# Encoder block on one core: weights of four stages moved to 112 bytes from the left factor

## The chip, the cores and the metric

The kernel runs on one core of a Trainium2 chip. The metric is device time in microseconds of one execution; the kernel before took 948.29 us (median of three runs, 947.97 to 948.39).

## The reference

One layer of an encoder, 256 tokens of width 2048, all in float32:

```python
h = rmsnorm(x, norm1_g)
q, k, v, u = split(h @ w_in)              # 12 q heads, 4 k/v heads of 128; u 512 wide
a = rmsnorm(window_attention(q, k, v, sink), attn_out_g)      # |t-s| <= 128, ALiBi, sink
f = rmsnorm(fourier_mix(u, w_fourier), fourier_out_g)         # Re(DFT2), then a map per group
x = x + concat([a, f]) @ w_out
h = rmsnorm(x, norm2_g)
gate, val = split(h @ w_up)               # 5504 columns each
gate = depthwise_conv3(gate, dw_w) + dw_b
x = x + (gelu(gate) * val) @ w_down
y = rmsnorm(x, normf_g)
```

## The kernel before, in words

Every large matmul is done in three parts to keep float32 precision: each operand is split into a rounded half `hi` (float32r) and the rest `lo`, and hi*hi, lo*hi and hi*lo are summed in PSUM. Weights come in units of 128 x 2048 values. `load` brings a unit to SBUF through SP's queue, three units ahead; `split` makes the halves two units ahead of their use, `hi` with a copy on ScalarE (ACT, line 168) and `lo` with a subtraction on VectorE (DVE, line 169). `parts_of` gives the halves their slots: three slots of 2176 elements for each of `hi` and `lo`, and inside the slot the 2048 values start at an offset that `shifts` names for the unit. Offsets count elements of 4 bytes.

TensorE takes two operands. The left factor is loaded into the array (LDWEIGHTS, PEld in the profile), then the other operand streams through it, up to 512 columns for one matmul. Two helpers use the weights in the two roles:

- `moving_weights` (lines 302 to 304) streams the weights, and the left factor is a 128-column piece of activations: `hT` for u and v, `cat` for the output projection, `act` for the late k tiles of the down projection. The first four k tiles of u (line 381) and the last k tiles of the down projection (`last_product`, lines 1190 to 1192) do the same with loops of their own.
- `still_weights` (line 319) takes the weights as left factor and streams the activations: q, k, gate and val.

The stages follow each other in an order that the program writes out by hand: u (units 0 to 3, `ps_u`), v (4 to 7, `ps_v`), q and k (16 units) with attention and Fourier work between them, the output projection (16 units, `ps_a` and `ps_ff`), gate and val (86 units) and between them the down projection. The down projection of the first 32 k tiles is done by seven products of blocks instead of eight (`split_product`, `by_parts`, lines 1051 to 1053, tiles `ps_P` and `ps_N`), where `hi` and `lo` stream and the operands `op_P`, `op_N` are left factors. The other k tiles are "late" (32 to 39, `ps_l`, two groups of four units) and "last" (40 to 42, `ps_e`, made by `split_last` and the line 168 splits).

Where the operands lie in SBUF is plain from the built program. The slots of `hi`, `lo`, `cat`, `act` and `op` start at byte 32 modulo 128, `hT` at byte 96. The table gives the start of the streamed operand minus the start of the left factor, modulo 128 bytes, before the change:

| matmuls | offset in the slot | distance |
|---|---|---|
| u, v | 16 elements (64 bytes) | 0 |
| q, k, gate, val | hi 0, lo 16 elements, as left factor | hi 64, lo 0 |
| output projection | 0 | 0 |
| products of the down projection | 28 elements (112 bytes) | 112 |
| late and last k tiles of the down projection | 0 | 0 |

Of the kernel before, what the change touches and what calls it, by code (L numbers as in the profile page):

```python
# [9 lines left out]
F32R = mybir.dt.float32r  # L10
# [3 lines left out]
P = 128  # L14
# [20 lines left out]
SHIFT = 16  # L35

PRODUCT_SHIFT = 28

V_G2, V_GA, V_GF, V_DW, V_DB, V_SINK = 0, 16, 28, 32, 161, 204
V_N = 216  # L40
# [52 lines left out]
def block_kernel(  # L93
# [26 lines left out]
    def f32(ap):  # L120
        return ap.bitcast(F32)
# [4 lines left out]

    units = [(w_u_x[i], 2048) for i in range(4)] + [(w_in[i], 2048) for i in range(20)]
    units += [(w_out[i], 2048) for i in range(16)]
    shifts = [(SHIFT, SHIFT)] * 8 + [(0, SHIFT)] * 16 + [(0, 0)] * 16
    n_front = len(units)  # L130
    items, up_index = ff_items(), {}
    for n, it in enumerate(items):
        if it[0] == "product":
            continue
        up_index[n] = len(units)
        if it[0] in ("gate", "val"):
            units.append((w_up[2 * it[1] + (it[0] == "val")], 2048))
            shifts.append((0, SHIFT))
            continue
        elif it[0] == "down":  # L140
            units.append((w_down_late[4 * it[1] + it[2]], 2048))
        else:
            units.append((w_down_last[it[1]], 512 * len(LAST)))
        shifts.append((0, 0))
    RAW = 3
    raws, halves = {}, {}

# [6 lines left out]
    def parts_of(i):  # L154
        halves[i] = tuple(
            wp.tile([P, 2176], F32R, tag=h, name=f"{h}{i}", bufs=3)[:, s : s + 2048]
            for h, s in zip(("hi", "lo"), shifts[i])
        )
        return halves[i]
# [44 lines left out]
    def u_part(k, o, n, m=1):  # L204

        rows = ux[k // 4][:, (k < 4) * U_HEAD :].rearrange("p (k c) -> p k c", k=4)
        return rows[:, k % 4 : k % 4 + m, o : o + n]
# [155 lines left out]
    for k in range(NK):  # L363
        c, q = k // 4, k % 4
        if q == 0:
            hi, lo = (t.rearrange("p (k c) -> p k c", k=4) for t in parts_of(c))
        n = 1 if c < 2 else 2
# [3 lines left out]
        if q % n == 0:  # L371
            w, h = u_part(k, 0, FW, n), hi[:, q : q + n, :]
# [416 lines left out]
    for n, (c, kq) in enumerate(OUT_ORDER):  # L789
        i = N_OUT + n  # L790
# [32 lines left out]
    fp = ctx.enter_context(tc.tile_pool(name="fp", bufs=2))  # L823
# [106 lines left out]
    def split_product(g, c, p):  # L930
# [5 lines left out]
            wp.tile([P, 2176], F32R, tag=h, name=f"{h}_{p}_{g}{c}", bufs=3)[  # L936
                :, PRODUCT_SHIFT : PRODUCT_SHIFT + 2048
            ]
# [192 lines left out]
    for n, it in enumerate(items):  # L1131
# [15 lines left out]
        if it[0] == "product":  # L1147
            kind, g, c, p = it
# [10 lines left out]
        else:  # L1159
            kind, g, c = it  # L1160
            hi, lo = halves.pop(up_index[n])
# [11 lines left out]
    i = up_index[n]  # L1173

    def split_last(c):
        raw, n = raws[i + c], 512 * len(LAST)
        hi = fp.tile([P, 2048], F32R, tag="rawd", name=f"hi{i + c}")
        lo = fp.tile([P, 2048], F32R, tag="rawd", name=f"lo{i + c}")
        halves[i + c] = (hi, lo)
        nc.scalar.activation(hi[:, 0:n], raw[:, 0:n], AF.Copy)  # L1180
        nc.vector.tensor_tensor(lo[:, 0:n], raw[:, 0:n], f32(hi[:, 0:n]), ALU.subtract)

    def last_product(c, b, o=0, n=512):
# [11 lines left out]
        last_post(c, b, ps, o, n)  # L1195

    split_last(3)
    for c in range(4):
        last_product(c, 0)
# [122 lines left out]
```

## Time and profile before

| what | value |
|---|---|
| median of three runs | 948.29 us |
| the profiled execution | 947.67 us |
| its span, first to last instruction | 945.9 us |
| TensorE busy, mean granted clock | 936.5 us (99%), 0.997 |
| weight loads, VectorE, ScalarE busy | 812.6, 749.6, 534.0 us |

In time the stages stand so, in us from the span's start: u to 27, v to 53, q, k and attention to 161, output projection to 256 (its first units between the last attention steps), gate, val and products to 845, late tiles from 845 to 867 and from 899 to 921, last tiles to 938, final norm and output to 946. The profile models the ends of matmuls, and they overlap in the array, so TensorE's pace is read from one start to the next.

### The profile page before, as it was taken

The numbers are of one execution on the slowest core, as the hardware profiler recorded it, in microseconds if no ns is written. First come the engines' busy times: TensorE is split into PE (matmuls) and PEld (weight loads), VectorE is DVE, ScalarE is ACT, GpSimd is POOL, SyncE is SP. The second block draws the span as 40 slices with busy tenths as digits, with TensorE's granted clock in tenths as the row PEclk, the third lists the DMA queues.
The fourth block names the chain that finished last, engine by engine and source line by source line (L and its number), as shares of the span: only waits on it lengthen the run. The fifth ranks groups of instructions, "written<-read, shape, count | busy, mean of one in ns | idle before, by whom it ended". The sixth has DMA issues, their size and how long they took to land.

```text
span 945.9 us, 12778 instructions
## 1 busy us (share of the span) xinstructions
PE 936.5 (99%) x5085; PEld 812.6 (86%) x5085; DVE 749.6 (79%) x935; ACT 534.0 (56%) x646; POOL 42.0 (4%) x57
## 2 busy tenths in 40 slices
PE   9999999999999999999999999999999999999996
PEld 7889998888888888888888888888888888888885
DVE  7758877666676689787898877988879979888776
ACT  7656766455454546556565555665556755553442
POOL 0000000000000000000000000000000000000002
PEclk9999999999999999999999999999999999999998
DMA  9854444446546675978778797877987697776542
GB/s 367 337 185 144 168 146 166 142 170 222 178 178 227 251 234 187 287 244 265 225 260 245 241 304 235 267 231 229 294 257 243 209 298 222 222 244 218 182 134 89
DMA packets 32108, 211.58 MB, mean 224 GB/s; under 512 B 3504, under 2 KB 4016, under 8 KB 7984
## 3 DMA queue, kind: packets, MB, share of 16 engines
q1 hardware_dynamic: 28448, 184.55, 52.6%
q0 software_dynamic: 3600, 26.22, 14.6%
q8 instruction: 40, 0.66, 0.3%
q14 instruction: 20, 0.16, 0.0%
HBM read 208.65 MB, written 2.10 MB: 223 GB/s over the span
## 4 chain that ended last, share of the span: by engine, by line
PE 98%; issue 1%; DMA 0%; DVE 0%; POOL 0%; ACT 0%; DVEq 0%; POOLq 0%; ACTq 0%
PE ps_gate L319 25%; PE ps_val L319 25%; PE ps_q L319 7%; PE ps_P L1051 3%; PE ps_P L1053 3%; PE ps_P L1052 3%; PE ps_a L304 2%; PE ps_k L319 2%; PE ps_a L302 2%; PE ps_a L303 2%; PE ps_N L1051 2%; PE ps_N L1053 2%; PE ps_N L1052 2%; PE ps_l L303 2%; PE ps_l L302 2%; PE ps_l L304 2%
## 5 line engine op out<-in xcount | busy, mean ns | idle before, releaser
L169 DVE TENSOR_TENSOR lo<-raw,hi 128x2048 fp32r<-128x2048 f32 (+1 forms) x133 | 302.6, 2275 | 54.3 <-ACT hi L168 54.3
L168 ACT ACTIVATE hi<-raw 128x2048 fp32r<-128x2048 f32 (+1 forms) x133 | 253.1, 1903 | 59.5 <-PE ps_l L303 24.9
L319 PE MATMUL ps_gate<-hU,hi 128*128 128x512 f32 x688 | 236.2, 389 | 0.0
L319 PE MATMUL ps_val<-hU,hi 128*128 128x512 f32 x688 | 236.2, 389 | 0.0
L319 PE MATMUL ps_gate<-hU,lo 128*128 128x256 f32 x688 | 189.9, 276 | 0.0
L319 PE MATMUL ps_val<-hU,lo 128*128 128x256 f32 x688 | 189.9, 276 | 0.0
L319 PEld LDWEIGHTS ps_gate<-hU,hi 128*128 128x128 f32 x688 | 129.2, 188 | 26.8
L319 PEld LDWEIGHTS ps_val<-hU,hi 128*128 128x128 f32 x688 | 129.1, 188 | 26.8
L319 PEld LDWEIGHTS ps_gate<-hU,lo 128*128 128x128 f32 x688 | 129.2, 188 | 1.1
L319 PEld LDWEIGHTS ps_val<-hU,lo 128*128 128x128 f32 x688 | 129.2, 188 | 1.1
L831 ACT ACTIVATE ft_g<-ps_gate 128x256 f32<-128x256 f32 x43 | 16.5, 384 | 120.1 <-PE ps_gate L319 119.9
L831 ACT ACTIVATE ft_v<-ps_val 128x256 f32<-128x256 f32 x43 | 16.5, 384 | 88.1 <-PE ps_val L319 88.1
L319 PE MATMUL ps_q<-hT,hi 128*128 128x512 f32 x192 | 66.2, 392 | 0.0
L319 PE MATMUL ps_q<-hT,lo 128*128 128x256 f32 x192 | 52.3, 277 | 0.0
L1053 PE MATMUL ps_P<-lo_P,op_P 128*128 128x512 f32 x128 | 49.8, 389 | 0.0
L1051 PE MATMUL ps_P<-hi_P,op_P 128*128 128x512 f32 x128 | 49.8, 389 | 0.0
L1052 PE MATMUL ps_P<-hi_P,op_P 128*128 128x512 f32 x128 | 49.8, 389 | 0.0
L943 DVE TENSOR_TENSOR lo_N<-sumw,hi_N 128x2048 fp32r<-128x2048 f32 x16 | 36.6, 2290 | 10.2 <-ACT hi_N L942 10.2
L319 PEld LDWEIGHTS ps_q<-hT,hi 128*128 128x128 f32 x192 | 35.7, 188 | 6.9
L302 PE MATMUL ps_a<-hi,cat 128*128 128x512 f32 x96 | 37.9, 395 | 0.0
L304 PE MATMUL ps_a<-lo,cat 128*128 128x512 f32 x96 | 37.5, 391 | 0.0
L833 DVE TENSOR_TENSOR fa_g<-ps_gate,ft_g 128x256 f32<-128x256 f32 x43 | 18.1, 421 | 24.3 <-ACT ft_g L831 24.3
(332 smaller groups left out, 1603.0 us busy)
## 6 DMA issues: line engine op xcount, KB each, us to landing
raw<-in_w_up SPq DMA_DIRECT2D x86, 1024.0 KB, 5.1
raw<-in_w_in SPq DMA_DIRECT2D x20, 1024.0 KB, 4.8
raw<-in_w_out SPq DMA_DIRECT2D x16, 1024.0 KB, 4.8
sumw<-in_w_down POOLq DMA_DIRECT2D x16, 1024.0 KB, 8.6
raw<-in_w_down_late SPq DMA_DIRECT2D x8, 1024.0 KB, 4.8
raw<-in_w_down_last SPq DMA_DIRECT2D x4, 768.0 KB, 4.2
ux<-in_w_u_x SPq DMA_DIRECT2D x3, 768.0 KB, 9.0
xs<-in_x SPq DMA_DIRECT2D x4, 512.0 KB, 16.3
```

Of the source, the lines that this page charges most:

```text
L168: nc.scalar.activation(hi[:, 0:n], raw[:, 0:n], AF.Copy)
L169: nc.vector.tensor_tensor(lo[:, 0:n], raw[:, 0:n], f32(hi[:, 0:n]), ALU.subtract)
L302: nc.tensor.matmul(ps, ah, wh, start=first and q == q0, stop=False)
L303: nc.tensor.matmul(ps, al, wh, start=False, stop=False)
L304: nc.tensor.matmul(ps, ah, wl, start=False, stop=last and q == q0 + len(kk) - 1)
L319: nc.tensor.matmul(ps[:, x], (hi, lo)[i][:, k * P : (k + 1) * P], hk(k)[:, x], start=n == 0 and k == 0, stop=n == len(order) - 1 and k == ...
L831: nc.scalar.activation(tmp, ps[:, S : 2 * S], AF.Copy)
L833: nc.vector.tensor_tensor(add, ps[:, 0:S], tmp, ALU.add)
L943: nc.vector.tensor_tensor(lo, src, f32(hi), ALU.subtract)
L1051: nc.tensor.matmul(ps, o[:, 0, p, :], hi[:, s], start=first and p == 0, stop=False)
L1052: nc.tensor.matmul(ps, o[:, 1, p, :], hi[:, s], start=False, stop=False)
L1053: nc.tensor.matmul(ps, o[:, 0, p, :], lo[:, s], start=False, stop=last and p == 3)
```

## The change

Every unit whose weights stream gets the offset that makes its distance 112 bytes. For u and v that is 44 elements (176 bytes from the slot's start, 112 from `hT` modulo 128), for the output projection and the late and last tiles 28 elements. The tiles of `split_last` are cut the same way. The gate, val, q and k units and the products are left as they are. Slots, their sizes and addresses, the order of instructions, transfers and waits are the same in both programs; the start of `hi` and `lo` differs in 849 matmuls, 42 ScalarE and 46 VectorE instructions, each time by 28 elements. For the last tile, `hi` and `lo` of `split_last`, the slots are those of `rawd`.

```diff
+FRONT_SHIFT = SHIFT + PRODUCT_SHIFT
...
-    shifts = [(SHIFT, SHIFT)] * 8 + [(0, SHIFT)] * 16 + [(0, 0)] * 16
+    shifts = [(FRONT_SHIFT, FRONT_SHIFT)] * 8 + [(0, SHIFT)] * 16
+    shifts += [(PRODUCT_SHIFT, PRODUCT_SHIFT)] * 16
...
-        shifts.append((0, 0))
+        shifts.append((PRODUCT_SHIFT, PRODUCT_SHIFT))
...
     def split_last(c):
         raw, n = raws[i + c], 512 * len(LAST)
-        hi = fp.tile([P, 2048], F32R, tag="rawd", name=f"hi{i + c}")
-        lo = fp.tile([P, 2048], F32R, tag="rawd", name=f"lo{i + c}")
+        hi, lo = (
+            fp.tile([P, 2048], F32R, tag="rawd", name=f"{h}{i + c}")[
+                :, PRODUCT_SHIFT : PRODUCT_SHIFT + n
+            ]
+            for h in ("hi", "lo")
+        )
```

## The prediction

> **What bounds the kernel now.** I read the page first, then the groups with their forms kept apart, then TensorE's timeline at the places that the change touches, then the busy times by stage.
>
> ```profile
> span 945.9 us, 12778 instructions
> ...
> PE 936.5 (99%) x5085; PEld 812.6 (86%) x5085; DVE 749.6 (79%) x935; ACT 534.0 (56%) x646; POOL 42.0 (4%) x57
> ...
> PEclk9999999999999999999999999999999999999998
> ...
> PE 98%; issue 1%; DMA 0%; DVE 0%; POOL 0%; ACT 0%; DVEq 0%; POOLq 0%; ACTq 0%
> ```
>
> TensorE is busy for 99% of the span, at full granted clock, and the chain that ended last is 98% TensorE. Beside the matmuls the weight loads (PEld) run for 86% of the span: nearly always one operand streams through the array while the next left factor is being read. So the kernel takes as long as its matmuls take from start to start, and a change of addresses can matter on one path above all: if it alters that step. The busy durations don't show the step, as matmuls overlap; the starts in the timeline do. First a product, whose streamed operand already lies 112 bytes (modulo 128) from its left factor:
>
> ```profile
> 360.84 0.39 PE L1051 MATMUL ps_P<-hi_P,op_P 128*128 128x512 f32 x1
> ...
> 363.33 0.39 PE L1053 MATMUL ps_P<-lo_P,op_P 128*128 128x512 f32 x1
> 363.56 0.39 PE L319 MATMUL ps_val<-hU,hi 128*128 128x512 f32 x1
> ```
>
> Twelve matmuls lie between 360.84 and 363.56: 2.72 / 12 = 226.7 ns each, from the first one on. Now the four places that the change moves, all at a distance of 0 modulo 128 so far: u, the output projection, and the late tiles of the down projection (v has the addresses of u).
>
> ```profile
> 10.60 0.39 PE L302 MATMUL ps_u<-hi,hT 128*128 128x512 f32 x1
> ...
> 13.32 0.39 PE L302 MATMUL ps_u<-hi,hT 128*128 128x512 f32 x1
> ...
> 219.35 0.39 PE L303 MATMUL ps_a<-hi,cat 128*128 128x512 f32 x1
> ...
> 238.62 0.40 PE L304 MATMUL ps_a<-lo,cat 128*128 128x512 f32 x1
> ...
> 845.00 0.39 PE L302 MATMUL ps_l<-hi,act 128*128 128x512 f32 x1
> ...
> 846.15 0.39 PE L304 MATMUL ps_l<-lo,act 128*128 128x512 f32 x1
> 846.38 0.39 PE L302 MATMUL ps_l<-hi,act 128*128 128x512 f32 x1
> ...
> 850.46 0.39 PE L302 MATMUL ps_l<-hi,act 128*128 128x512 f32 x1
> ```
>
> u: 12 matmuls in 2.72 us, 226.7 ns. Output projection: 85 in 19.27 us, 226.7 ns. Late tiles: 18 from 846.38 to 850.46 in 4.08 us, 226.7 ns. In steady flow distance 0 and distance 112 have the same step to a tenth of a nanosecond. That is the row on which the forecast rests.
>
> What remains above this step shows in the groups: the mean is 389 ns where nothing is in the way, and larger where a matmul's successor came late.
>
> ```profile
> L1051 PE MATMUL ps_P<-hi_P,op_P 128*128 128x512 f32 x128 | 49.8, 389 | 0.0
> ...
> L302 PE MATMUL ps_a<-hi,cat 128*128 128x512 f32 x96 | 37.9, 395 | 0.0
> L304 PE MATMUL ps_a<-lo,cat 128*128 128x512 f32 x96 | 37.5, 391 | 0.0
> L303 PE MATMUL ps_a<-hi,cat 128*128 128x512 f32 x96 | 37.3, 389 | 0.0
> ...
> L302 PE MATMUL ps_l<-hi,act 128*128 128x512 f32 x64 | 24.9, 389 | 0.0
> ...
> L302 PE MATMUL ps_ff<-hi,cat 128*128 128x512 f32 x32 | 12.6, 393 | 0.0
> L304 PE MATMUL ps_v<-lo,hT 128*128 128x512 f32 x32 | 12.5, 391 | 0.0
> ...
> L1190 PE MATMUL ps_e<-hi,act 128*128 128x512 f32 x21 | 8.2, 389 | 0.0
> ...
> L381 PE MATMUL ps_u<-hi,hT 128*128 128x512 f32 x16 | 4.8, 424 | 0.3 <-ACT hT L256 0.3
> ```
>
> **The change part by part.** No instruction, wait, transfer or slot is added, removed or moved: the slots keep their places, and 28 elements are added to the start of hi and lo where they are used. That reaches 849 matmuls: u 96, v 96, output projection 384, late tiles 192, last tiles 81. It also reaches the ACT and DVE instructions that write those halves.
>
> *The steady step.* At the new distance the nearest row is the product: 226.7 ns, against 226.7 now. 849 x 0 = 0. The bounds from both sides are these same rows, so a tenth of a nanosecond each, 0.1 us in all. The low bits of the product's addresses are also what u, v, out and the late tiles get: the late and out operands sit at byte 16 modulo 128 with left factors at 32, exactly as in the products; u and v sit at 80 with hT at 96.
>
> One rule bears on this step. The Trainium skill, "TensorE: Matmul & The Clock Gate", section "Back-to-back issue gap", gives N/2.4 + 2.5 ns for one warm matmul, 216 ns at 512 columns, while the trace has 226.7. If the 11 ns between them came from the distance of the operands and 112 bytes removed it, the 831 wide matmuls of the change would give 9 us. The trace disagrees with that reading: products at 112 bytes take 226.7 too.
>
> *The slow restarts.* After the transposes and other small fp32 matmuls the stream needs some matmuls to come back to its step:
>
> ```profile
> 205.15 0.47 PE L302 MATMUL ps_a<-hi,cat 128*128 128x512 f32 x1
> 205.46 0.39 PE L303 MATMUL ps_a<-hi,cat 128*128 128x512 f32 x1
> ...
> 207.54 0.39 PE L303 MATMUL ps_a<-hi,cat 128*128 128x512 f32 x1
> ```
>
> The first step is 0.31 us, and the next nine take 2.08 us, 231 ns each, 4.4 over the floor. At the entry to the late tiles five steps from 845.00 to 846.15 plus one to 846.38 take 1.38 us, 0.02 over six floors of 226.7. All such time within the change's reach is read from the group means over 389: ps_a 96 x 6 + 96 x 2 ns = 0.77 us, ps_ff 32 x 4 = 0.13, ps_v 32 x 2 = 0.06, ps_l and ps_e nothing that shows; together 1.0 us. (The 16 x 35 ns of ps_u at the start are waits for hT and its data and do not hang on this address.) No row has a restart at 112 bytes after fp32 transposes. The product shown starts at the floor at once, but it comes from wide matmuls. So the restarts are worth from -1.0 us (all vanish) to +1.0 us (they double). I take 0, because both the product's and the out projection's own steady rows say that the address is not what sets the step, and what precedes a restart stays as it is.
>
> *The narrow last matmuls.* The last tile is cut to 256 columns, 18 of them:
>
> ```profile
> 935.51 0.28 PE L1190 MATMUL ps_e<-hi,act 128*128 128x256 f32 x1
> ...
> 937.54 0.28 PE L1192 MATMUL ps_e<-lo,act 128*128 128x256 f32 x1
> ```
>
> 17 steps in 2.03 us, 119.4 ns, where half of 226.7 would be 113.3; 17 x 6.1 = 0.10 us. Bounded by losing that excess or doubling it: -0.1 to +0.1, taken as 0.
>
> *The splits.* The halves are written at another offset: 42 ACT and 46 DVE instructions.
>
> ```profile
> L169 DVE TENSOR_TENSOR lo<-raw,hi 128x2048 fp32r<-128x2048 f32 x130 | 297.3, 2287 | 52.7 <-ACT hi L168 52.7
> L168 ACT ACTIVATE hi<-raw 128x2048 fp32r<-128x2048 f32 x130 | 248.6, 1912 | 50.5 <-PE ps_l L303 15.9 <-PE ps_a L303 13.5 <-PE ps_ff L303 9.0
> ...
> L943 DVE TENSOR_TENSOR lo_N<-sumw,hi_N 128x2048 fp32r<-128x2048 f32 x16 | 36.6, 2290 | 10.2 <-ACT hi_N L942 10.2
> L942 ACT ACTIVATE hi_N<-sumw 128x2048 fp32r<-128x2048 f32 x16 | 30.6, 1910 | 0.0
> ```
>
> L942 and L943 already write at byte 112 of the slot: 1910 and 2290 ns against 1912 and 2287 for the units at 0 and 64. Plus 3 ns on DVE, minus 2 on ACT. These are covered by TensorE in all stages, thinnest here:
>
> ```profile
> 4.00:26.00 22.00, 21.71 (x94) 17.79 (x94) 19.00 (x31) 16.01 (x27) 0.00 (x0) 1.00 1.02 406
> ...
> 844.00:867.00 23.00, 23.00 (x103) 19.01 (x102) 21.46 (x24) 9.01 (x7) 0.00 (x0) 1.00 0.66 229
> ```
>
> (stretch and its length, then PE, PEld, DVE, ACT, POOL busy, granted clock, DMA share and GB/s). In the late stage DVE has 1.5 us left of 23 while TensorE has no gap. Should 3 ns come to each split, it is nothing beside that; if the cover were gone, 46 x 3 = 0.14 us. In the first stage it is the DMA that is full (1.02), and no transfer touches hi or lo.
>
> *Sum.* Step 0, restarts 0 (-1.0 to +1.0), narrow ones 0 (-0.1 to +0.1), splits 0 (to +0.14). The profiled execution took 947.67 us, 1.8 more than its span; it stays at 947.7, and that execution is 0.62 under the median of the runs. So I forecast the median: 948.3 us.
>
> **The rivals.** *Slower: the new distance collides wherever the stream is not in the product's rhythm.* The mechanism: the load of the next left factor reads while the streamed operand is read, and at 112 bytes the restarts never settle. Its place is u, v and the output projection, 576 matmuls, which stand among fp32 transposes and attention work that products never follow, and where (u, v) the left factor is hT, which no product has. Price: the 4.4 ns of the restart above, kept on all: 576 x 4.4 = 2.5 us, 950.8 us. It decides from 1.9 us / 576 = 3.3 ns per matmul. For it: no row shows a restart at 112. Against it: the product starts at the floor at once, and u and v have hardly a restart. 4 in 100.
>
> *Faster: distance 0 costs part of the step itself.* It decides from 1.9 us / 849 = 2.2 ns per matmul, which gives 946.4 us or less. For it: only that 226.7 is not proven to be the least. Against it: the product's row at 112. 2 in 100. By the Trainium skill's 216 ns it would be 939 us.
>
> *The restarts alone heal*: 947.3 us, a real gain that lies inside my forecast's bounds; perhaps 15 of its 94.
>
> That the distance doesn't become 112 is excluded: the slots' addresses in the built program give 112 modulo 128 on each of the 849.
>
> **How the numbers follow.** 0.2% is 1.9 us, about what a measurement of this kernel can tell from no change. No change within that: 0.94, the whole forecast with both ends of the restarts. Slower 0.04, faster 0.02 from the rivals. The range takes 948.3 with the restarts' 1.0 to each side and some 0.3 for the splits, narrow matmuls and the spread of the runs (947.97 to 948.39): 947.0 to 949.6.
>
> **What would show it.** Right: 226.7 ns from start to start in the same windows of u, out and late tiles; means of 389 for ps_l and ps_u L302; out means still near 395 on L302 of ps_a; DVE and ACT splits within 5 ns. The restarts are judged by ps_a's L302 and L304 means alone: 389 is all healed, 401 doubled. Wrong: a step that differs by over 2 ns in any of the four places, or TensorE gaps that end on a split.

## The result, and the profile after

The changed kernel is slower: 949.81 us (median of 22 runs, 949.23 to 950.56) against 948.12 us (median of 22 runs, 947.62 to 949.74) for the kernel before beside it. The ratio is 1.0018, with a 95% interval of 1.0012 to 1.0024. That is 1.7 us; the forecast was 948.3, with a range up to 949.6. The two profiled executions lie further apart, spans of 945.9 and 948.5 us, because 0.7 of their 2.6 us is chance: the six matmuls at the very start took 2.71 us in this execution and 1.88 in the one before. In the executions of this study they took between 1.7 and 2.7 us, whatever the address: 2.65 in one with u at distance 0 (`before_break` below), 1.68 in one with u at 112 (`entry_wide`). In the slow starts the steps are 426 ns, while the profile gives the granted clock as 1.00; what causes them is not shown.

First the groups of the profile after, forms kept apart. The lines 304 to 306 are the old 302 to 304, the lines 170 and 171 the old 168 and 169.

```profile
PE 939.2 (99%) x5085; PEld 813.0 (86%) x5085; DVE 749.6 (79%) x935; ACT 533.9 (56%) x646; POOL 42.0 (4%) x57
...
L171 DVE TENSOR_TENSOR lo<-raw,hi 128x2048 fp32r<-128x2048 f32 x130 | 297.3, 2287 | 53.0 <-ACT hi L170 53.0
L170 ACT ACTIVATE hi<-raw 128x2048 fp32r<-128x2048 f32 x130 | 248.5, 1912 | 51.4 <-PE ps_l L305 15.8 <-PE ps_a L305 14.0 <-PE ps_ff L305 9.3
L304 PE MATMUL ps_a<-hi,cat 128*128 128x512 f32 x96 | 38.1, 397 | 0.0
L305 PE MATMUL ps_a<-hi,cat 128*128 128x512 f32 x96 | 37.7, 393 | 0.0
L306 PE MATMUL ps_a<-lo,cat 128*128 128x512 f32 x96 | 37.7, 392 | 0.0
L304 PE MATMUL ps_l<-hi,act 128*128 128x512 f32 x64 | 24.9, 389 | 0.0
```

The splits are what they were, 2287 and 1912 ns, and TensorE's two waits, at the start, are those of before (1.0 us each, and 0.3 and 0.2 for `hT`). TensorE has as many matmuls and is busy 2.7 us longer. In the output projection the means moved from 395, 389, 391 to 397, 393, 392. That looks like little, and no mean shows the step. The timeline does: u, the output projection and the late tiles of the kernel after (start, duration, instruction).

```profile
12.08 0.39 PE L304 MATMUL ps_u<-hi,hT 128*128 128x512 f32 x1
...
12.78 0.39 PE L304 MATMUL ps_u<-hi,hT 128*128 128x512 f32 x1
...
14.16 0.39 PE L304 MATMUL ps_u<-hi,hT 128*128 128x512 f32 x1
...
219.69 0.39 PE L304 MATMUL ps_a<-hi,cat 128*128 128x512 f32 x1
...
240.71 0.39 PE L305 MATMUL ps_a<-hi,cat 128*128 128x512 f32 x1
...
847.68 0.39 PE L304 MATMUL ps_l<-hi,act 128*128 128x512 f32 x1
...
852.44 0.39 PE L304 MATMUL ps_l<-hi,act 128*128 128x512 f32 x1
```

u: nine matmuls from 12.08 to 14.16 in 2.08 us, 231.1 ns each. Output projection: 91 matmuls from 219.69 to 240.71 in 21.02 us, 231.0 ns. Late tiles: 21 in 4.76 us, 226.7 ns, from the first one on. So one program at one distance has two steps. A triple, three matmuls on one left factor, takes 693 ns in u and the output projection and 680 ns in the late tiles; the products, whose address was not touched, have 680 too. Below, a stream is "fast" at 680 per triple and "slow" at 693; which of the two it is in is called its phase.

Stage by stage, from the starts of the seventh u matmul, of the first work behind v, of the output projection and of the gate units, before and then after (the late tiles begin at 845.00 before and at 847.68 after, the last matmul at 937.54 and 940.09):

```profile
6.52 0.39 PE L381 MATMUL ps_u<-hi,hT 128*128 128x512 f32 x1
53.02 0.27 PE L286 MATMUL ps_spread<-diag,ones 128*128 128x128 f32 x1
161.42 0.40 PE L302 MATMUL ps_a<-hi,cat 128*128 128x512 f32 x1
256.09 0.39 PE L319 MATMUL ps_gate<-hU,hi 128*128 128x512 f32 x1
```

```profile
7.22 0.40 PE L383 MATMUL ps_u<-hi,hT 128*128 128x512 f32 x1
54.35 0.38 PE L288 MATMUL ps_spread<-diag,ones 128*128 128x128 f32 x2
162.74 0.39 PE L304 MATMUL ps_a<-hi,cat 128*128 128x512 f32 x1
258.69 0.39 PE L321 MATMUL ps_gate<-hU,hi 128*128 128x512 f32 x1
...
940.09 0.28 PE L1198 MATMUL ps_e<-lo,act 128*128 128x256 f32 x1
```

| stage | before | after | difference |
|---|---|---|---|
| to the seventh u matmul (chance) | 6.52 | 7.22 | +0.70 |
| rest of u, v | 46.50 | 47.13 | +0.63 |
| q, k, attention | 108.40 | 108.39 | -0.01 |
| output projection | 94.67 | 95.95 | +1.28 |
| gate, val, products | 588.91 | 588.99 | +0.08 |
| late and last tiles | 92.54 | 92.41 | -0.13 |

Without the first row the sum is +1.85 us, which agrees with the medians (+1.69). The change costs in u, v and the output projection, and brings a tenth in the late tiles.

### The profile page after: what moved, and what is told of

Its sections match the earlier page's. It is cut to its first block, busy times and chain, and to the rows that moved or that the text cites. A ratio compares the mean times of both kernels' runs of the same rounds, so it can differ in the third digit from the quotient of the medians.

```text
span 948.5 us, 12778 instructions
## 1 busy us (share of the span) xinstructions
PE 939.2 (99%) x5085; PEld 813.0 (86%) x5085; DVE 749.6 (79%) x935; ACT 533.9 (56%) x646; POOL 42.0 (4%) x57
## 4 chain that ended last, share of the span: by engine, by line
PE 98%; issue 1%; DMA 0%; DVE 0%; POOL 0%; ACT 0%; DVEq 0%; POOLq 0%; ACTq 0%
PE ps_gate L321 25%; PE ps_val L321 25%; PE ps_q L321 7%; PE ps_P L1054 3%; PE ps_P L1055 3%; PE ps_P L1053 3%; PE ps_a L305 2%; PE ps_a L306 2%; PE ps_a L304 2%; PE ps_k L321 2%; PE ps_N L1054 2%; PE ps_N L1055 2%; PE ps_N L1053 2%; PE ps_l L306 2%; PE ps_l L304 2%; PE ps_l L305 2%
## 5 line engine op out<-in xcount | busy, mean ns | idle before, releaser
L304 PE MATMUL ps_a<-hi,cat 128*128 128x512 f32 x96 | 38.1, 397 | 0.0
L305 PE MATMUL ps_a<-hi,cat 128*128 128x512 f32 x96 | 37.7, 393 | 0.0
```

What stands on the lines that cost most here:

```text
L304: nc.tensor.matmul(ps, ah, wh, start=first and q == q0, stop=False)
L305: nc.tensor.matmul(ps, al, wh, start=False, stop=False)
```

## The experiments

A break, in what follows, is a run of small matmuls between two streams: fp32 ones (transposes, sums), or the attention's with 256 columns, which are float32r. The theory that formed from these rows: the distance does not set a step, it sets whether a stream *returns* to the fast one. At distance 0 it returns within some ten matmuls from whatever went before. At 112 it keeps what it was entered with: fast behind gate, val and products, slow behind breaks. The rival: the stage decides, through the left factor (`hT` and `cat` against `act` and `op`) or its other traffic, and the way into the stream plays no part.

**One part at a time.** u and v alone:

```diff
+FRONT_SHIFT = SHIFT + PRODUCT_SHIFT
...
-    shifts = [(SHIFT, SHIFT)] * 8 + [(0, SHIFT)] * 16 + [(0, 0)] * 16
+    shifts = [(FRONT_SHIFT, FRONT_SHIFT)] * 8 + [(0, SHIFT)] * 16 + [(0, 0)] * 16
```

> Only u and v at 112, all else as before. Theory (a second rhythm): at 112 bytes a stream that starts after a break runs for good in triples of 693 ns (225, 231, 237) where the old distance comes back to 680 (226, 227, 227). Then u has 32 triples at 693 and v some 20, up to the Fourier matmuls: 52 x 13 ns = 0.7 us, ratio 1.0007; the output projection stays as before, with 680 after its restarts. Rival (the start): the 0.8 us that u lost at its beginning in the changed kernel's profile, in steps of 426 ns at a cold clock, belong to the change as well: 1.5 us, 1.0016, and again some five steps of 426 ns.

The output projection alone:

```diff
-    shifts = [(SHIFT, SHIFT)] * 8 + [(0, SHIFT)] * 16 + [(0, 0)] * 16
+    shifts = [(SHIFT, SHIFT)] * 8 + [(0, SHIFT)] * 16 + [(PRODUCT_SHIFT, PRODUCT_SHIFT)] * 16
```

> Only the output projection at 112. Theory: all its 128 triples run at 693, 1.7 us more than a pure 680, less the 0.4 us of restarts that the old distance already pays: +1.3 us, ratio 1.0014; u and v at 680. Rival (interplay with the earlier stages: the slow rhythm is handed down from u): the output projection comes back to 680 within a unit and the time is that of before.

The late and last tiles alone:

```diff
-        shifts.append((0, 0))
+        shifts.append((PRODUCT_SHIFT, PRODUCT_SHIFT))
...
+            fp.tile([P, 2048], F32R, tag="rawd", name=f"{h}{i + c}")[
+                :, PRODUCT_SHIFT : PRODUCT_SHIFT + n
+            ]
...
```

> Only the late and last tiles at 112. Theory: these streams are entered from still units in the fast rhythm, so they stay at 680; the two slow entries (0.05 us) and half the excess of the narrow last matmuls (0.05 us) go: -0.1 us, ratio 0.9999, not to be told from no change by time, but from the steps. Rival (112 bytes is slower in itself in any stage but the products): 91 triples x 13 ns = 1.2 us, 1.0013.

Against 948.10 us for the kernel before on the same chip: u and v 948.57 (ratio 1.0005, 0.9996 to 1.0013), output projection 949.43 (1.0013, 1.0004 to 1.0022), late and last 947.75 (0.9997, 0.9988 to 1.0006). Only the output projection is told from no change by its interval; the others are read from their triples. In the second kernel the triples of the output projection are slow all through, but for single ones at an entry or an end, while its u and v are fast behind the start; in the first it is the other way round, except that v turns fast behind the Fourier step's 256-column float32r matmuls, which stand before v's last unit. The late tiles are fast from the first matmul: the 0.05 us lost at their entry is gone, and about half of the 0.106 us of the narrow ones. The three differences add up to +1.45 us, near the change's +1.69. The rival of the first run, that the slow start belongs to the change, asked for +1.5 us from u and v; they cost 0.47.

**The other way round: the products at distance 0.**

```diff
-PRODUCT_SHIFT = 28
+PRODUCT_SHIFT = 0
```

> The kernel before with the products at distance 0 instead of 112. Theory: in steady flow both distances have the step of 226.7 ns; an entry at distance 0 costs what the late tiles' two entries cost, 25 ns, and there are some 56 entries: up to +1.4 us, ratio 1.0015. Rival (the distance means nothing to a stream that is entered from a still unit): no change, 1.0000, and products that start at 226.7 ns.

950.64 us against 948.10, ratio 1.0027 (1.0017 to 1.0037). One product of this kernel and the entry to the unit behind it:

```profile
361.38 0.39 PE L1051 MATMUL ps_P<-hi_P,op_P 128*128 128x512 f32 x1
...
362.08 0.40 PE L1051 MATMUL ps_P<-hi_P,op_P 128*128 128x512 f32 x1
...
364.13 0.39 PE L319 MATMUL ps_val<-hU,hi 128*128 128x512 f32 x1
```

The twelve take 2.75 us, not 2.72; the triples are 695, 690, 680, 680. So distance 0 does come back, and pays 25 ns for it. The gate or val unit behind it takes 5.46 instead of 5.44 us, another 22 ns, which nothing had foreseen. 56 products x 47 ns = 2.6 us, the 2.54 measured. Each pass between gate/val and a stream at distance 0 has this price; at 112 it has none. Where streams begin behind gate and val units, 112 is the better place, and the late tiles gain for that reason.

**A break in front of the late tiles.** Eight fp32 matmuls on constants before each group of late tiles, and before one product in the middle; once on top of the late kernel above (late tiles at 112), once on the kernel before (late tiles at 0). Both programs do all the reference's work besides.

```diff
+            if c == 0:
+                for _ in range(8):
+                    nc.tensor.matmul(ps[0][:, 0:P], ones, ones, start=True, stop=True)
...
+                if (g, c, p) == (1, 0, "N3"):
+                    for _ in range(8):
+                        nc.tensor.matmul(ps[:, 0:P], ones, ones, start=True, stop=True)
```

> The kernel with only the late and last tiles at 112, and eight added fp32 matmuls of 128 columns (ones by ones, overwritten after) before the first late unit of each group and before one product (N3 of the second block group, first half). Theory (112 keeps the rhythm that a stream is entered with): after the first triple of about 775, the late stream of each group stays at 693 through all four units, 32 triples, and the product's four triples are at 693; all other products stay at 680. Rival (the slow rhythm comes from what runs beside in the early stages: full DMA, attention work on the other engines): the late stream and the product come back to 680 within some ten matmuls.

> The same added matmuls in the kernel before, where the late tiles are at distance 0 and the products at 112. Theory (distance 0 pulls back to the fast rhythm, 112 does not): the late streams go 775, 691, 697, 684 and then 680, as the output projection does after its transposes; the product N3 stays at 693 for its four triples. Rival (early stages): both come back.

963.87 us at 112 and 962.55 at 0, one execution each, beside 947.80 for the kernel before. The late tiles, second matmul of the first group to the first gate matmul behind it, at 112 and then at 0:

```profile
857.66 0.39 PE L303 MATMUL ps_l<-hi,act 128*128 128x512 f32 x1
...
879.61 0.39 PE L319 MATMUL ps_gate<-hU,hi 128*128 128x512 f32 x1
```

```profile
858.33 0.39 PE L303 MATMUL ps_l<-hi,act 128*128 128x512 f32 x1
...
879.89 0.39 PE L319 MATMUL ps_gate<-hU,hi 128*128 128x512 f32 x1
```

95 steps each: 21.95 us at 112, 231.1 ns; 21.56 us at 0, 226.9 ns. With a break in front of it, the stage that was fast at 112 is slow through all 32 triples, and at 0 it returns. The rival by stage and left factor falls. The surprise is what the break before the product did, in the chain of waits of the kernel with late tiles at 112:

```profile
505.22 5.44 PE ps_val L319 x32
510.66 1.78 PE ps_N L1156 x16
...
515.22 5.60 PE ps_gate L319 x32
...
523.59 5.60 PE ps_val L319 x32
```

The unit before the break takes 5.44 us. Behind it, the product (at 112) and all gate and val units are slow, 5.60 us each, to the end; in the kernel with late tiles at 0, 42 gate and val units are slow up to the late tiles, and the first gate unit behind those takes 5.46 us, the next 5.44. Of the 16.1 us, the three breaks of 1.78 us are 5.3, and 48 gate and val units x 0.16 us are 7.7; the rest lies in the slow products and late tiles. One short break was never paid back: everything behind it kept the phase that it was handed.

**Is it the distance, or where the weights start?** The products at distance 0 in place of 112 were to be brought back to 112 by moving the left factors instead; the slots had to become smaller for that.

```diff
-PRODUCT_SHIFT = 28
+PRODUCT_SHIFT = 0
+LEFT = 4
...
-            wp.tile([P, 2176], F32R, tag=h, name=f"{h}{i}", bufs=3)[:, s : s + 2048]
+            wp.tile([P, 2080], F32R, tag=h, name=f"{h}{i}", bufs=3)[:, s : s + 2048]
...
-        o = fp.tile([P, 2, 4, P], F32R, tag=f"op_{name}", name=f"op_{name}", bufs=1)
+        o = fp.tile([P, 1056], F32R, tag=f"op_{name}", name=f"op_{name}", bufs=1)
+        o = o[:, LEFT : LEFT + 1024].rearrange("p (a b c) -> p a b c", a=2, b=4)
...
-            wp.tile([P, 2176], F32R, tag=h, name=f"{h}_{p}_{g}{c}", bufs=3)[
+            wp.tile([P, 2080], F32R, tag=h, name=f"{h}_{p}_{g}{c}", bufs=3)[
```

> Products with the streamed halves at offset 0 and the left factors op moved up by 16 bytes instead: the distance is again 112 modulo 128, but no stream starts at byte 16 any more (slots are 2080 elements long to make room, all addresses the same modulo 128). Theory (the distance counts): entries at 226.7 ns, time of the kernel before, ratio 1.000. Rival (the absolute start of the stream counts): as with products at 0: slow entries of 25 ns at each product and each unit behind it, ratio 1.0027.

965.47 us, ratio 1.0187 (1.0173 to 1.02), for a reason of its own. Rows of its chain:

```profile
427.51 5.45 PE ps_gate L320 x32
...
435.76 5.55 PE ps_val L320 x32
...
452.44 5.65 PE ps_val L320 x32
```

Slots of 2176 elements are 17 x 512 bytes apart, so all three slots had the same low address bits; slots of 2080 elements (8320 bytes) differ by 128 bytes modulo 512 from one to the next, and gate and val units now take 5.45, 5.55 or 5.65 us. So address bits above the 128 bytes that the distances are counted by matter as well; the products' left factors now differ by multiples of 128 bytes modulo 512 among each other too, and the question asked was not answered by this run. It does answer another. In it u, v and the output projection still stand at 0 modulo 128, but by the addresses in the built program, in each of their units one of `hi` and `lo` stands at 0 and the other at 128 modulo 256. Their triples no longer return to 680: most repeat 687 or 700, or go to and fro between 691 and 696. A distance of 0 modulo 128 is not enough. In the kernel before, u and v stand at 256 modulo 512 and the output projection at 0, with `hi` and `lo` alike, and both return.

**Other distances** for u, v and the output projection: 64, 16, 32 and 96 bytes; the edit is that of the first two experiments, with 16, 4, 8 and 24 elements added to the offsets of the kernel before.

> u, v and the output projection at distance 64 (16 elements more), the rest as before. Theory says only that the distance decides whether a stream returns to 680: if only distances near 0 pull back, all triples of u, v and the output projection are at 693 as at 112; if 112 alone is special, they come back within some ten matmuls as at 0.

> u, v and the output projection with halves 16 bytes past the left factor, instead of 16 short of it (112 modulo 128). Theory leaves open which distances pull back. If the sign does not matter: triples of 693 throughout, +1.9 us. If only the sign of 112 does harm: back to 680 within ten matmuls.

> The same at distance 32. At 64 bytes the triples stayed at 687 everywhere, at 112 at 693, at 0 they return to 680. If the steady loss grows with the distance from 0: between 680 and 687. If it goes in steps of 64 bytes: 680 or 687.

> The same at distance 96. If the steady loss grows with the distance modulo 128: some 690 a triple. If 96 counts as 32 short of the left factor: the value of distance 32.

One execution each: 948.79 us at 64 (beside 947.80), 949.61 at 16, 950.64 at 32 and 950.56 at 96 (beside 948.04). One unit of the output projection, 24 matmuls, from its first to the next unit's first, in this order: distance 0 (before), 64, 112 (after), 16, 32.

```profile
227.96 0.39 PE L302 MATMUL ps_ff<-hi,cat 128*128 128x512 f32 x1
...
233.40 0.39 PE L302 MATMUL ps_a<-hi,cat 128*128 128x512 f32 x1
```

```profile
228.59 0.39 PE L302 MATMUL ps_ff<-hi,cat 128*128 128x512 f32 x1
...
234.08 0.39 PE L302 MATMUL ps_a<-hi,cat 128*128 128x512 f32 x1
```

```profile
230.09 0.39 PE L304 MATMUL ps_ff<-hi,cat 128*128 128x512 f32 x1
...
235.63 0.39 PE L304 MATMUL ps_a<-hi,cat 128*128 128x512 f32 x1
```

```profile
229.40 0.40 PE L302 MATMUL ps_ff<-hi,cat 128*128 128x512 f32 x1
...
234.96 0.40 PE L302 MATMUL ps_a<-hi,cat 128*128 128x512 f32 x1
```

```profile
230.24 0.40 PE L302 MATMUL ps_ff<-hi,cat 128*128 128x512 f32 x1
...
235.84 0.40 PE L302 MATMUL ps_a<-hi,cat 128*128 128x512 f32 x1
```

5.44, 5.49, 5.54, 5.56 and 5.60 us; 96 bytes gives 5.60 too. Of the distances tried, only 0 gets back to the fast step in these stages, and the loss does not grow steadily with the distance. Nor do the four turn fast where 112 does: behind the Fourier step's matmuls, v's last unit is fast at 112 and stays near 687 per triple at 64 bytes, 695 at 16 and 700 at 32 and 96. At 64 bytes the output projection's weights start at the same address modulo 512 as those of u in the kernel before, which are fast, and still the step is 229 ns: that speaks for the distance and against the start alone.

**The first form of the theory falls.** It said that only breaks make a stream at 112 slow. So, from the kernel after, the units right behind a break went back to distance 0, and only units that follow a settled unit kept 112.

```diff
-    shifts = [(FRONT_SHIFT, FRONT_SHIFT)] * 8 + [(0, SHIFT)] * 16
-    shifts += [(PRODUCT_SHIFT, PRODUCT_SHIFT)] * 16
+    shifts = [(SHIFT, SHIFT)] * 8 + [(0, SHIFT)] * 16 + [(0, 0)] * 16
+    for n in (1, 2, 3, 4, 5):
+        shifts[n] = (FRONT_SHIFT, FRONT_SHIFT)
+    for n in (5, 8, 10, 11, 12, 14, 15):
+        shifts[24 + n] = (PRODUCT_SHIFT, PRODUCT_SHIFT)
```

> As the changed kernel (late and last tiles at 112), but a unit of u, v or the output projection that starts behind a break keeps the old distance; 112 is given only to units that another wide unit precedes without a break: units 1 to 3 of u, the first two of v, and units 5, 8, 10, 11, 12, 14, 15 of the output projection. Theory (112 keeps the rhythm of the entry): all these twelve units run at 680 a triple, where the same units at the same distance ran at 693 in the changed kernel; the time is that of the kernel with the late tiles alone, ratio 0.9997 to the kernel before. Rival (112 is slow in these stages, whatever the entry): their 96 triples stay at 693, 96 x 13 ns = 1.3 us, ratio 1.001 or more.

948.99 us against 948.04, ratio 1.0010 (1.0001 to 1.0019): still slow. The entry from a unit at 0 to a unit at 112 (the line shown first is the last triple at 0):

```profile
211.12 0.39 PE L307 MATMUL ps_a<-hi,cat 128*128 128x512 f32 x1
...
211.80 0.39 PE L307 MATMUL ps_a<-hi,cat 128*128 128x512 f32 x1
...
212.48 0.39 PE L307 MATMUL ps_a<-hi,cat 128*128 128x512 f32 x1
...
216.64 0.39 PE L307 MATMUL ps_a<-hi,cat 128*128 128x512 f32 x1
```

0.68 us per triple up to 212.48, then 18 matmuls in 4.16 us, 231.1 ns. A fast predecessor is not enough; a settled stream at distance 0 hands over the slow phase. That leaves gate, val and products, and the Fourier step's matmuls before v's last unit, as the ones that hand over the fast one.

**The entry alone.** So the last two kernels are the kernel after with matmuls of another kind put in front of output projection units 0, 1, 4 and 6 and nothing moved there: eight pairs as in a gate unit (`cat` as left factor, 512 and 256 columns of `hT`), or, as the control, twelve wide matmuls at distance 0. In the first kernel the first late unit is at distance 0 besides.

```diff
+            if n in (0, 1, 4, 6):
+                for k in range(8):
+                    nc.tensor.matmul(ps[0], cat[0][:, 0:P], hk(k), start=True, stop=True)
+                    nc.tensor.matmul(ps[0][:, 0:S], cat[0][:, 16 : 16 + P], hk(k)[:, 0:S], start=True, stop=True)
...
-        shifts.append((PRODUCT_SHIFT, PRODUCT_SHIFT))
+        late0 = it[:3] == ("down", 0, 0)
+        shifts.append((0, 0) if late0 else (PRODUCT_SHIFT, PRODUCT_SHIFT))
```

```diff
+            if n in (0, 1, 4, 6):
+                for k in range(12):
+                    nc.tensor.matmul(ps[0], cat[0][:, 0:P], cat[1], start=True, stop=True)
```

> The changed kernel with two edits. (1) Eight pairs of added matmuls stand before four output units that begin a sum (0, 1, 4 and 6), laid out like those of a still unit: left factor in cat at the addresses that weights have there, 512 and then 256 columns of hT streaming, results overwritten. (2) The first late unit of group 0 goes back to distance 0, the other late units stay at 112. Theory, second form (112 keeps the phase it is entered with; a settled still stream hands over the good phase, a break or a stream at distance 0 the bad one): the output units 0, 1, 4, 5 and 6 run at 680 a triple at 112 bytes, 40 triples that were at 693; late unit 0 runs at 680 at distance 0, units 1 to 3 at 693 though they run at 680 in the changed kernel, and the gate and val units behind them at 5.60 us instead of 5.44. Rival (the stage decides: 112 is slow in the front and fast in the down projection): output units at 693 as before, late units at 680.

> The control: the changed kernel with twelve added wide matmuls before the same four output units, at distance 0 (cat streaming, cat as left factor). Theory, second form: the added ones settle at 226.7 ns, and the output units behind them go to 693 all the same. Rival (any settled stream ahead of the unit is enough): output units 0, 1, 4, 5 and 6 at 680.

962.61 and 960.87 us (one execution each, beside 948.04). The added matmuls alone, by 226.7 and 113.3 ns, are some 10.9 us in both. The first kernel, behind the pairs, and in its late tiles behind the unit at distance 0:

```profile
196.99 0.39 PE L305 MATMUL ps_ff<-hi,cat 128*128 128x512 f32 x1
...
207.64 0.40 PE L307 MATMUL ps_a<-lo,cat 128*128 128x512 f32 x1
...
863.52 0.39 PE L305 MATMUL ps_l<-hi,act 128*128 128x512 f32 x1
...
880.15 0.39 PE L322 MATMUL ps_gate<-hU,hi 128*128 128x512 f32 x1
```

and the control, at the same place:

```profile
197.41 0.39 PE L304 MATMUL ps_ff<-hi,cat 128*128 128x512 f32 x1
...
202.27 0.39 PE L304 MATMUL ps_a<-hi,cat 128*128 128x512 f32 x1
```

Behind the pairs, 47 steps at 112 bytes in 10.65 us, 226.6 ns: the output projection at 112 is fast, which it nowhere was in the kernel after. Behind the wide matmuls, 21 in 4.86 us, 231.4 ns. And in the late tiles, which were fast at 112 before, one unit at distance 0 in front makes the other three slow: 72 matmuls in 16.63 us, 231.0 ns; the gate and val units behind them take 5.60 us, as expected. Same weights, same addresses, same stage; only what runs ahead differs. One expectation failed: unit 0 stayed slow. There the pairs themselves ran slowly (350 instead of 340 ns), behind the scores' matmuls of the attention, and handed that on. The same is to be seen in the kernel after, where the first gate matmuls behind the slow output projection take 0.35 us per pair until the next fp32 transposes, at 262.88: the 0.08 us of the table.

## Why the prediction was wrong

**What failed is the step "The slow restarts".** It took 0, with -1.0 and +1.0 us as bounds, "because both the product's and the out projection's own steady rows say that the address is not what sets the step". Both rows were right, and did not bear on the question: the steady row at 112 came only from streams that gate and val units precede, the steady row at 0 only from the distance that returns by itself. No row showed a stream at 112 behind fp32 matmuls; the text said so, and then priced it as if the restart would end as it ends at 0. The amount itself, 1.0 us, came from the means of durations; by the starts, the output projection lost 0.89 us over 680 per triple before the change, and about half of that lies in the first steps behind breaks, which are as long at 112, so that only some 0.4 us were in reach. In place of that step the runs show no restart but a state: some +0.6 us in u and v, +1.3 in the output projection, without an end until something else changes the phase. The bounds were wrong for the same reason: twice the restart's 1.0 us is no bound for a loss that grows with the length of the stream.

**The steady step.** Its floor, 226.7 ns, was right for the late tiles and wrong as a step for u, v and the output projection (231.1). The place that the prediction named for it, the timeline, showed it at once, and its sign of being wrong, a step over 2 ns off, is there in three of the four places; the place that it named for the restarts, means of 389 or 401 on ps_a, did not, since the slow phase appears there as 397, 393 and 392.

**The narrow last matmuls and the splits.** About -0.05 us against 0 within ±0.1, and 2287 and 1912 ns: as forecast. No wait or transfer moved.

**The rivals.** The slower one was right in what it said of the restarts, "at 112 bytes the restarts never settle", in its place, u, v and the output projection, and in its 4.4 ns per matmul (231.1 - 226.7); that two reads collide, its mechanism, is not shown by any run. Its sum, 2.5 us and 950.8, was too high by what the old kernel already lost in restarts (about 0.4 us), by v's last unit, which the Fourier step's matmuls reset, and by the tenth that the late tiles gain. It got 4 in 100 because "the product starts at the floor at once, and u and v have hardly a restart"; the first spoke for entries from gate and val units alone, and the second for distance 0 alone. The faster rival had nothing to it: no triple at any distance was under 679 ns, 226.3 per matmul. The Trainium skill ("TensorE: Matmul & The Clock Gate", section "Back-to-back issue gap") gives 216 ns for one warm matmul of 512 columns; no stream of any run here comes to that.

**A rule that would have forecast no change.** The Trainium skill's page "SBUF — State Buffer", section "Who interferes with whom", gives TensorE two independent read ports, one for the streamed operand and one for the weight load, and says that it never waits on anyone. The step of these matmuls does depend on where the two operands lie towards each other, 226.7 to 233 ns. The runs do not show whether the reads are what collides.

**Open.** What the state consists of, inside the memory or the array, was not measured. That the distance counts modulo 128 was an assumption, and the run with smaller slots speaks against it; a count modulo 256 would fit the streams that return, and was not tested by itself. Why some short matmuls leave the slow phase behind (scores, the added fp32 ones) and others the fast one (the Fourier step's, the transposes ahead of val units) is not settled. In the built program the scores stand at distance 0, like the wide matmuls that hand over the slow phase, and the Fourier step's at 96 modulo 128; whether that decides was not tested. The best version seen is the kernel with only the late and last tiles at 112 bytes, 947.75 us; its gain of 0.35 us is not told from none, and the steps of its profile account for 0.13.

## What to carry to other kernels

A steady row shows the step of a stream only for the way in which that stream was entered; before moving an address, find a row with the new address *and* the same predecessor, and where there is none, price the loss over the whole length of the stream and not as a short restart. When TensorE is the bound, read start-to-start sums over three matmuls in the timeline, since group means hide two per cent. In this kernel the better place depends on what runs before: distance 0 for streams behind breaks, the distance that keeps the phase (here 112 bytes) for streams between long runs of gate and val units.

## What of the hardware was unexpected

- The step of a 512-column matmul depends on the streamed operand's distance from the left factor: over 24 matmuls 5.44 us at 0 bytes, 5.49 at 64, 5.54 at 112, 5.56 at 16, 5.60 at 32 and 96, in the output projection.
- The state is inherited over units: one break of 1.78 us made each of the gate and val units behind it 5.60 us long instead of 5.44. In one kernel that lasted to the end; in the other for 340 us, until a stream at distance 0 came, behind which they were back at 5.44 after one unit.
- Distance 0 has a price of its own between gate and val units, 25 ns at its entry and 22 ns in the unit behind.
